# Reciprocal roots of both token tiles taken ahead of the rotations, in a two-layer hybrid decoder

## The chip, the core and the metric

The kernel runs on one core of a Trainium2 chip. The metric is the device time of one execution in microseconds (us), lower is better. PE is the matrix engine (TensorE), DVE the vector engine, ACT the scalar engine, POOL the GpSimd engine and SP the sync engine, which here only issues transfers. Each engine works through its own list of instructions in order and waits at semaphores for what the others deliver.

## What is computed

Two decoder layers over 256 tokens and 1024 channels in float32. Each layer has two attention branches (mixer A with a top-k selection of keys by a small indexer, mixer B with two softmax maps whose weighted difference is used), a gated merge, a convolutional feed-forward block and a gated embedding. Cut to what matters here:

```
qa, ka, va, qi, ki, wi, qb, kb, vb, gate_a, gate_b = split(rms_norm(h) @ w_in)
qa = rope(rms_norm(qa, g_qa));  ka = rope(rms_norm(ka, g_ka))     # heads of 64
qi = rope(qi);  ki = rope(ki);  wi = wi * H_I**-0.5 * D_I**-0.5
qb = rope(rms_norm(qb, g_qb));  kb = rope(rms_norm(kb, g_kb))
iscore = sum_h relu(qi . ki) * wi, causal;   sel = top 64 keys of each query
o_a = softmax over the selected keys (qa . ka / 8) @ va
o_b = (softmax(q1 . k1 / 8) - lam * softmax(q2 . k2 / 8)) @ vb;   o_b = rms_norm(o_b)
mix = sigmoid(gate_a) * (o_a @ w_branch_a) + sigmoid(gate_b) * (o_b @ w_branch_b)
h = h + mix @ w_out;   h = h + conv_ffn(rms_norm(h));   h = h + ple_gate * (p @ w_ple_proj)
```

The norm of a head is a sum of 64 squares and a reciprocal root. The rotation (`rope`) is linear, so the factor can be put on before or after it.

## The kernel before

**Tiles.** The 256 tokens are two tiles of 128 partitions, i = 0 and 1. All weights come in 128 chunks of 128x1024 per layer. SP issues their transfers (`raw`), ACT rounds each to a high part `wh` (line 164), DVE takes the rest `wl = raw - wh` (line 179). Every product of activations and weights is then three matmuls on PE (lines 352 to 354): `u_hi wh`, `u_hi wl`, `u_lo wh`. Here those three are called a triple. A chunk serves four triples in the projections.

**The side work.** While PE streams the projections and gates of a layer, the attention is done between its triples. Each piece is a Python generator (`index_side`, `heads_side`, `select_side`, `mixer_b`, `mixer_a`, `o_side`). A planner (`Side.tick`, called after every four triples) lets each generator go on to its next `yield`, when its own estimates of the engines' loads allow it. The three numbers of a `yield` are those estimates, for PE, DVE and ACT. They do not reach the chip. They only decide behind which triples a piece's instructions are written, and each engine then runs its list in exactly that order. Below, a visit is such a place in PE's list, named by the number of triples of the layer that stand ahead of it.

**Around the change.** A projection's result is read by ACT from PSUM to `prq` (line 477). `heads_side` works on it, for queries of mixer B, keys of mixer B (`nm == "kb"`) and queries of mixer A. For each tile `head_ss` squares on ACT (line 414) and sums on DVE (line 415, `hss`); `rpow` makes the reciprocal root on POOL (lines 261 and 262, `pw` and `rq`); `rope_rows` rotates with four DVE instructions (lines 402, 405 twice, 409). Queries take their factor later, in the exponential. Keys are multiplied by it on DVE (line 576) right behind the rotation of their tile. Then PE transposes both tiles (line 425, eight 128x128), and ACT copies them to `qT` (line 427).

**What comes behind.** `maps` multiplies queries and keys (mask at line 596, products at 628 or 633), reduces the maxima on DVE (lines 601 and 602, `mx`, `nb`), and takes exponentials on ACT (line 605, eight for a pair of maps). For mixer B, DVE then combines the two softmax maps (lines 642 to 645, writing `pe`), PE transposes `pe` (line 620), and multiplies by the values (line 656). The maps, the transposes and the products with values share four PSUM buffers named `tp`. `select_side` runs eight top-k rounds on DVE (lines 545 and 547), two for each `yield`.

Of the kernel before, what the change touches and what calls it, by code (L numbers as in the profile page):

```python
# [9 lines left out]
F32 = mybir.dt.float32  # L10
F32R = mybir.dt.float32r
BF16 = mybir.dt.bfloat16
AF = mybir.ActivationFunctionType
# [4 lines left out]
P = 128  # L18
# [7 lines left out]
EPS = 1e-6  # L26
# [83 lines left out]
def decoder_kernel(ctx: ExitStack, tc: tile.TileContext, x, pT, ws, fc, tb, gf, rope, out):  # L110
    nc = tc.nc
# [146 lines left out]
    def rpow(dst, src, mul, add):  # L258
        n = src.shape[-1]
        t = sm.tile([P, 8], F32, name="pw", bufs=4)  # L260
        nc.gpsimd.tensor_scalar(t[:, :n], src, mul, add, op0=ALU.mult, op1=ALU.add)
        nc.gpsimd.tensor_tensor(dst, t[:, :n], mhalf[:, :n], op=ALU.pow)  # L262
# [148 lines left out]
    def head_ss(src, n):  # L411
        sq = sm.tile([P, 8, 64], F32, name="sq", **T2)[:, :n, :]
        ss = sm.tile([P, 8], F32, name="hss", bufs=3)
        nc.scalar.activation(sq, src, AF.Square)
        nc.vector.reduce_sum(ss[:, :n], sq, axis=AX.X)
        return ss[:, :n]
# [25 lines left out]
    for l in range(DEPTH):  # L442
# [43 lines left out]

        def index_side(pi):
            kk, iq, wvs = [], [], []
            for i in range(2):
                v = pi[i]  # L490
                nc.scalar.activation(va[:, i, :], v[:, 64:128], AF.Copy)
                kki = sm.tile([P, 4, 64], F32, name="kk")
                rope_rows(kki[:, 0:2, :], v[:, 0:64].unsqueeze(1), 1, rt["ka"], i, dup=True)
                rope_rows(kki[:, 2:4, :], v[:, 384:448].unsqueeze(1), 1, rt["i"], i, dup=True)
                rk = sm.tile([P, 1], F32, name="rk")
                rpow(rk, head_ss(v[:, 0:64].unsqueeze(1), 1), 1.0 / 64, EPS)
                iqi = sm.tile([P, 4, 64], F32, name="iq")
                rope_rows(iqi, v[:, 128:384].rearrange("p (a b) -> p a b", b=64), 4, rt["i"], i)
                nc.scalar.activation(kki[:, 0:2, :], kki[:, 0:2, :], AF.Copy, scale=rk)
                wv = sm.tile([P, 4], F32, name="wv")  # L500
                nc.vector.tensor_scalar(wv, v[:, 448:452], 0.0625, None, op0=ALU.mult)
                kk.append(kki.rearrange("p a b -> p (a b)"))
                iq.append(iqi.rearrange("p a b -> p (a b)"))
                wvs.append(wv)
                yield 0.0, 2.8, 0.0
            pt = ps_tp.tile([P, 2, L], F32, name="tp")
            for j in range(2):
                for i in range(2):
                    nc.tensor.transpose(pt[:, j, i * P:(i + 1) * P], kk[i][:, j * P:(j + 1) * P], ident)
            nc.scalar.activation(kT, pt[:, 0, :], AF.Copy)  # L510
            nc.scalar.activation(kiT, pt[:, 1, :], AF.Copy)
            iqT = sm.tile([P, 2, L], F32, name="iqT", **T2)
            transposed(iq, 2, iqT)
            yield 0.9, 0.0, 1.2
            rels = []
            for i in range(2):
                S = P * (i + 1)
                rel = b4("rel")[:, :, :S]
                ps = [ps_tp.tile([P, 2, L], F32, name="tp") for _ in range(2)]
                for b in range(2):  # L520
                    for r in range(2):
                        nc.tensor.matmul(ps[r][:, b, :S], iqT[r * 64:(r + 1) * 64, b, i * P:(i + 1) * P],
                                         kiT[r * 64:(r + 1) * 64, :S], start=True, stop=True)
                for r in range(2):
                    nc.scalar.activation(rel[:, r:4:2, :], ps[r][:, :, :S], AF.Relu)
                rels.append(rel)
                yield 0.85 * (i + 1), 0.0, 0.9
            side.spawn(select_side(rels, wvs), P_TOPK)
# [32 lines left out]

        def heads_side(pr, nm, is_q):

            rows, rq = [], []
            for i in range(2):
                v = pr[i].rearrange("p (a b) -> p a b", b=64)
                q = sm.tile([P, 512], F32, name="qr", **T2)
                q3 = q.rearrange("p (a b) -> p a b", b=64)
                r_ = sm.tile([P, 8], F32, name="rq", bufs=6)
                if is_q:  # L570
                    rope_rows(q3, v, 8, rt[nm], i)
                    rpow(r_, head_ss(v, 8), 1.0, 64 * EPS)
                else:
                    rpow(r_, head_ss(v, 8), 1.0 / 64, EPS)
                    rope_rows(q3, v, 8, rt[nm], i)
                    nc.vector.tensor_mul(q3, q3, r_.unsqueeze(2).broadcast_to([P, 8, 64]))
                rows.append(q)
                rq.append(r_.rearrange("p (b r) -> p r b", r=2))
                yield 0.0, (2.8 if nm == "kb" else 2.2), 0.0
            rqs[nm] = rq  # L580
            qT[nm] = b4("qT")
            transposed(rows, 4, qT[nm])
            yield 0.9, 0.0, 1.0
            flags.add(nm)
# [459 lines left out]
```

## Time and profile before

| | before |
|---|---|
| median of three runs | 796.73 us (794.17 to 796.83) |
| the profiled execution | 797.8 us, of which 796.0 us are the span from the first to the last instruction |
| PE busy | 783.4 us, 98% of the span |
| DVE busy | 589.3 us, 74% |
| ACT busy | 503.5 us, 63% |
| POOL busy | 163.8 us, 21% |
| granted PE clock, mean | 0.999 |

All times below are from the one profiled execution and count from its first instruction. A busy share is an average: where engines work for one another in a chain, a wait can stand in a short stretch though the engine is far from full over the whole span.

### The profile page before, as it was taken

How to read it: one execution, taken by the hardware profiler on the slowest of the kernel's cores; microseconds unless marked ns; L12 is line 12 of the kernel's file. 1: busy time of each engine (PE TensorE's matmuls, PEld its weight loads, DVE VectorE, ACT ScalarE, POOL GpSimd, SP SyncE). 2: the span in 40 equal slices, each digit the busy share in tenths (PEclk: the TensorE clock that was granted, in tenths of full speed). 3: DMA queues.
4: the chain of work that ended last, by engine and by line, in shares of the span. 5: the costliest groups of instructions: out<-in, count | busy, mean ns of one | idle time of the engine just before them, and what ended most of it. 6: DMA issues, size and time to landing. Idle time of an engine off the chain costs nothing.

```text
span 796.0 us, 11725 instructions
## 1 busy us (share of the span) xinstructions
PE 783.4 (98%) x4049; PEld 646.7 (81%) x4049; DVE 589.3 (74%) x1130; ACT 503.5 (63%) x887; POOL 163.8 (21%) x162
## 2 busy tenths in 40 slices
PE   8999999999999999999999999999999999999997
PEld 6877876787888888888888778778878888888887
DVE  5987987677777778854686889768677777785643
ACT  6766657455877777643666486565468777774541
POOL 0240300010344442000123213000104444410000
PEclk9999999999999999999999999999999999999999
DMA  8654453474455556646365344446545555558421
GB/s 321 211 172 146 131 190 131 146 233 137 159 190 182 192 194 210 230 159 220 133 205 165 121 145 159 158 133 191 192 137 182 189 181 192 182 183 291 167 98 54
DMA packets 40332, 139.51 MB, mean 175 GB/s; under 512 B 4560, under 2 KB 5968, under 8 KB 40272
## 3 DMA queue, kind: packets, MB, share of 16 engines
q1 hardware_dynamic: 39408, 136.91, 51.4%
q10 hardware_dynamic: 864, 1.84, 0.8%
q8 instruction: 32, 0.52, 0.3%
q14 instruction: 28, 0.23, 0.1%
HBM read 137.69 MB, written 1.05 MB: 174 GB/s over the span
## 4 chain that ended last, share of the span: by engine, by line
PE 87%; DVE 5%; ACT 4%; POOL 1%; issue 1%; DMA 1%; SPq 0%; DVEq 0%; ACTq 0%; POOLq 0%
PE tp L821 21%; PE acc L352 11%; PE acc L354 11%; PE acc L353 11%; PE tp L822 10%; PE acc L905 5%; PE acc L903 5%; PE acc L904 5%; DVE wl L179 2%; ACT pe L605 2%; PE tp L315 2%; PE tp L620 1%; PE tp L699 1%; PE tp L656 1%; POOL rq L262 1%
## 5 line engine op out<-in xcount | busy, mean ns | idle before, releaser
L164 ACT ACTIVATE wh<-raw 128x1024 fp32r<-128x1024 f32 x254 | 264.7, 1058 | 37.1 <-PE acc L905 25.2
L821 PE MATMUL tp<-u,wh 128*128 128x512 f32 x704 | 249.6, 399 | 2.2 <-DVE u L787 2.2
L179 DVE TENSOR_TENSOR wl<-raw,wh 128x1024 fp32r<-128x1024 f32 x178 | 213.9, 1220 | 24.4 <-ACT wh L164 24.1
L822 PE MATMUL tp<-u,wl 128*128 128x256 f32 x704 | 197.7, 281 | 0.0
L821 PEld LDWEIGHTS tp<-u,wh 128*128 128x128 f32 x704 | 132.3, 188 | 36.1 <-DVE u L787 3.3
L352 PE MATMUL acc<-wh,u 128*128 128x512 f32 (+1 forms) x336 | 133.8, 398 | 0.0
L822 PEld LDWEIGHTS tp<-u,wl 128*128 128x128 f32 x704 | 133.0, 189 | 0.0
L354 PE MATMUL acc<-wh,u 128*128 128x512 f32 (+1 forms) x336 | 130.5, 388 | 0.0
L353 PE MATMUL acc<-wl,u 128*128 128x512 f32 (+1 forms) x336 | 130.5, 388 | 0.0
L176 POOL TENSOR_TENSOR wl<-raw,wh 128x512 fp32r<-128x512 f32 x76 | 98.5, 1296 | 149.4 <-DVE wl L175 71.5
L836 DVE SCALAR_TENSOR_TENSOR cv<-tp,fc,cv 128x255 f32<-128x255 f32 (+1 forms) x176 | 84.1, 478 | 3.1
L831 DVE TENSOR_TENSOR tp<-tp,cl 128x256 f32<-128x256 f32 x88 | 38.0, 432 | 50.9 <-ACT cl L829 50.9
L352 PEld LDWEIGHTS acc<-wh,u 128*128 128x128 f32 x336 | 63.1, 188 | 13.2 <-issue 0.7
L354 PEld LDWEIGHTS acc<-wh,u 128*128 128x128 f32 x336 | 63.1, 188 | 12.8
L353 PEld LDWEIGHTS acc<-wl,u 128*128 128x128 f32 x336 | 63.2, 188 | 11.7 <-DVE wl L179 0.2
L903 PE MATMUL acc<-wh,g 128*128 128x512 f32 x176 | 68.9, 391 | 0.0
L904 PE MATMUL acc<-wl,g 128*128 128x512 f32 x176 | 68.5, 389 | 0.0
L905 PE MATMUL acc<-wh,g 128*128 128x512 f32 x176 | 68.5, 389 | 0.0
L832 ACT ACTIVATE cv<-tp,fc 128x256 f32<-128x256 f32 x88 | 49.7, 565 | 24.5 <-DVE tp L831 24.0
L276 POOL TENSOR_SCALAR sst<-ss 128x2 f32<-128x2 f32 (+1 forms) x8 | 5.6, 699 | 259.2 <-ACT junk L268 259.1
L829 ACT ACTIVATE cl<-tp 128x256 f32<-128x256 f32 x88 | 33.8, 384 | 33.6 <-PE tp L822 33.3
L175 DVE TENSOR_TENSOR wl<-raw,wh 128x514 fp32r<-128x514 f32 x76 | 52.7, 693 | 0.0
(180 smaller groups left out, 1051.5 us busy)
## 6 DMA issues: line engine op xcount, KB each, us to landing
raw<-ws SPq DMA_DIRECT2D x254, 512.0 KB, 3.4
raw<-ws SPq DMA_DIRECT2D x4, 256.0 KB, 5.0
gb<-gf ACTq DMA_DIRECT2D x2, 512.0 KB, 4.5
h<-x SPq DMA_DIRECT2D x2, 256.0 KB, 4.3
h<-x SPq DMA_DIRECT2D x1, 512.0 KB, 6.6
px<-pT ACTq DMA_DIRECT2D x2, 256.0 KB, 2.8
out<-h SPq DMA_DIRECT2D x2, 256.0 KB, 2.8
out<-h SPq DMA_DIRECT2D x4, 128.0 KB, 1.8
```

The lines of the kernel that those rows point to most:

```text
L164: nc.scalar.activation(wh, raw, AF.Copy)
L176: nc.gpsimd.tensor_tensor(wl[:, b], raw[:, b], wh[:, b].bitcast(F32), op=ALU.subtract)
L179: nc.vector.tensor_sub(wl, raw, wh.bitcast(F32))
L352: nc.tensor.matmul(o, a, wh, start=q == 0, stop=False)
L353: nc.tensor.matmul(o, a, wl, start=False, stop=False)
L354: nc.tensor.matmul(o, b, wh, start=False, stop=q == nk - 1)
L821: nc.tensor.matmul(acc, wh[:, k, :], u.pair(k), start=k == 0, stop=False)
L822: nc.tensor.matmul(acc[:, 0, :], wl[:, k, :], u.hi(k), start=False, stop=k == KD - 1)
L836: nc.vector.scalar_tensor_tensor(c[:, sh:], pu[:, :L - sh], w[:, 2 - sh:3 - sh], c[:, sh:], op0=ALU.mult, op1=ALU.add)
L903: nc.tensor.matmul(acc[i], a, wh, start=k == 0, stop=False)
L904: nc.tensor.matmul(acc[i], a, wl, start=False, stop=False)
L905: nc.tensor.matmul(acc[i], b, wh, start=False, stop=k == NF - 1)
```

## The change

For mixer B's keys the squares, sums and reciprocal roots of both tiles are now asked for ahead of both rotations, and the multiplication by the root becomes a stage of its own, for both tiles together, behind a `yield` after the second rotation. In `index_side` the roots of both tiles' keys likewise stand ahead of the first rotation. Queries keep their order, and only their estimates in `yield` change. No arithmetic is added or dropped.

```diff
         def index_side(pi):
             kk, iq, wvs = [], [], []
+            rks = [sm.tile([P, 1], F32, name="rk") for _ in range(2)]
+            for rk, v in zip(rks, pi):
+                rpow(rk, head_ss(v[:, 0:64].unsqueeze(1), 1), 1.0 / 64, EPS)
             for i in range(2):
 ...
-                rk = sm.tile([P, 1], F32, name="rk")
-                rpow(rk, head_ss(v[:, 0:64].unsqueeze(1), 1), 1.0 / 64, EPS)
 ...
-                nc.scalar.activation(kki[:, 0:2, :], kki[:, 0:2, :], AF.Copy, scale=rk)
+                nc.scalar.activation(kki[:, 0:2, :], kki[:, 0:2, :], AF.Copy, scale=rks[i])
 ...
         def heads_side(pr, nm, is_q):
 
-            rows, rq = [], []
+            vs = [t.rearrange("p (a b) -> p a b", b=64) for t in pr]
+            rows = [sm.tile([P, 512], F32, name="qr", **T2) for _ in range(2)]
+            q3s = [q.rearrange("p (a b) -> p a b", b=64) for q in rows]
+            rs = [sm.tile([P, 8], F32, name="rq", bufs=6) for _ in range(2)]
+            rq = [r_.rearrange("p (b r) -> p r b", r=2) for r_ in rs]
+            if not is_q:
+                for r_, v in zip(rs, vs):
+                    rpow(r_, head_ss(v, 8), 1.0 / 64, EPS)
             for i in range(2):
-                v = pr[i].rearrange("p (a b) -> p a b", b=64)
-                q = sm.tile([P, 512], F32, name="qr", **T2)
-                q3 = q.rearrange("p (a b) -> p a b", b=64)
-                r_ = sm.tile([P, 8], F32, name="rq", bufs=6)
+                rope_rows(q3s[i], vs[i], 8, rt[nm], i)
                 if is_q:
-                    rope_rows(q3, v, 8, rt[nm], i)
-                    rpow(r_, head_ss(v, 8), 1.0, 64 * EPS)
+                    rpow(rs[i], head_ss(vs[i], 8), 1.0, 64 * EPS)
+                    yield 0.0, 2.7, 0.0
                 else:
-                    rpow(r_, head_ss(v, 8), 1.0 / 64, EPS)
-                    rope_rows(q3, v, 8, rt[nm], i)
+                    yield 0.0, 2.2 + 1.1 * (1 - i), 0.0
+            if not is_q:
+                for q3, r_ in zip(q3s, rs):
                     nc.vector.tensor_mul(q3, q3, r_.unsqueeze(2).broadcast_to([P, 8, 64]))
-                rows.append(q)
-                rq.append(r_.rearrange("p (b r) -> p r b", r=2))
-                yield 0.0, (2.8 if nm == "kb" else 2.2), 0.0
+                yield 0.0, 1.3, 0.0
             rqs[nm] = rq
             qT[nm] = b4("qT")
             transposed(rows, 4, qT[nm])
```

Four lines are added, so the lines behind the diff move by four: 576 becomes 582, 596 becomes 600, 605 becomes 609, 620 becomes 624, 628 becomes 632.

The planner reacts. **DVE, the keys of mixer B in the first layer**, from the sum of squares on: `m_...` are the halves of a rotation, `sc` the indexer's scores. Before:

```order
L415 TENSOR_REDUCE hss<-sq 128x8
L402 TENSOR_TENSOR m_668<-prq,rt_kb 128x512
L405 TENSOR_TENSOR m_669<-prq,rt_kb 128x8x32 x2
L409 TENSOR_TENSOR qr<-m_668,m_669 128x512
L576 TENSOR_TENSOR qr<-qr,rq 128x512
L179 TENSOR_TENSOR wl<-raw,wh 128x1024
L535 SCALAR_TENSOR_TENSOR sc<-rel,wv,cm 128x128
L538 SCALAR_TENSOR_TENSOR sc<-rel,wv,sc 128x128 x3
L179 TENSOR_TENSOR wl<-raw,wh 128x1024
```

And with the change, from the second tile's rotation on (both sums and the first rotation stand ahead of it, with the first tile's scores and two splits `wl` between):

```order
L402 TENSOR_TENSOR m_726<-prq,rt_kb 128x512
L405 TENSOR_TENSOR m_727<-prq,rt_kb 128x8x32 x2
L409 TENSOR_TENSOR qr<-m_726,m_727 128x512
L179 TENSOR_TENSOR wl<-raw,wh 128x1024
L536 SCALAR_TENSOR_TENSOR sc<-rel,wv,cm 128x256
L539 SCALAR_TENSOR_TENSOR sc<-rel,wv,sc 128x256 x3
L179 TENSOR_TENSOR wl<-raw,wh 128x1024
L582 TENSOR_TENSOR qr<-qr,rq 128x512 x2
L179 TENSOR_TENSOR wl<-raw,wh 128x1024
L546 MAX m_797<-sc 128x8
```

The multiplication no longer stands behind its own rotation. Two splits and the scores of both tiles have moved ahead of the second one, and top-k rounds, which stood behind the maps of mixer B before, follow soon after it.

**PE, the same layer, where the first transposes of `pe` stand.** Before, at the visit behind 96 triples, ten of them stood alone:

```order
L352 MATMUL acc<-wh,u 128x512
L353 MATMUL acc<-wl,u 128x512
L354 MATMUL acc<-wh,u 128x512
L620 MATMUL tp<-ident,pe 128x128 x10
L352 MATMUL acc<-wh,u 128x512
```

With the change, at the same visit:

```order
L352 MATMUL acc<-wh,u 128x512
L353 MATMUL acc<-wl,u 128x512
L354 MATMUL acc<-wh,u 128x512
L425 MATMUL tp<-ident,qr 128x128 x8
L624 MATMUL tp<-ident,pe 128x128 x4
L600 LDWEIGHTS identb
L600 MATMUL tp<-cmb,identb 128x2x128
```

The keys of mixer B are transposed behind 80 triples of the first layer instead of 72, and 76 of the second instead of 68 (counted from the first triple of the layer). The first maps still come four triples later. In the first layer the second pair of maps is now split over two later visits, the first map of it behind the four transposes of `pe`; in the second layer the second pair still stands four triples behind the first pair, and `pe` follows twelve triples later, with mixer A's query transposes ahead of it.

**ACT, the first layer, what stands around the exponentials** (`pe,sums`), with the change:

```order
L477 ACTIVATE prq<-acc,rstd 128x512 x2
L427 ACTIVATE qT<-tp 128x512 x2
L164 ACTIVATE wh<-raw 128x1024
L414 ACTIVATE sq<-prq 128x512
L609 ACTIVATE pe,sums<-tp,nb,rq 128x256 x4
L609 ACTIVATE pe,sums<-tp,nb,rq 128x128 x4
L164 ACTIVATE wh<-raw 128x1024
L414 ACTIVATE sq<-prq 128x512
L164 ACTIVATE wh<-raw 128x1024 x2
```

The squares of mixer A's second query tile stand behind eight exponentials and a split; before, the squares of its first tile stood so behind sixteen, and those of the second behind two more splits.

## Rows read from the trace of the kernel before

**Rows 1.** The page: span, and PE's busy time.

```profile
span 796.0 us, 11725 instructions
...
PE 783.4 (98%) x4049; PEld 646.7 (81%) x4049; DVE 589.3 (74%) x1130; ACT 503.5 (63%) x887; POOL 163.8 (21%) x162
```

**Rows 2.** PE's waits: line, awaited, us in total, times, longest.

```profile
PE tp L425 <- DVE qr L576: 1.3, 2, 1.0
PE tp L596 <- ACT pe L605: 0.9, 3, 0.5
```

**Rows 3.** PE's timeline, first layer: start us, us, instructions [idle before].

```profile
46.51 1.09 PE L425 MATMUL tp<-ident,qr 128*128 128x128 f32 x8
47.35 0.47 PE L352 MATMUL acc<-wh,u 128*128 128x512 f32 x1
...
61.09 0.28 PE L425 MATMUL tp<-ident,qr 128*128 128x128 f32 x1
...
62.31 0.47 PE L352 MATMUL acc<-wh,u 128*128 128x512 f32 x1
...
65.16 0.39 PE L596 MATMUL tp<-cmb,identb 128*128 128x256 bf16 x2
...
66.55 0.39 PE L596 MATMUL tp<-cmb,identb 128*128 128x256 bf16 x2
...
67.52 0.50 PE L352 MATMUL acc<-wh,u 128*128 128x512 f32 x1
...
70.41 0.59 PE L596 MATMUL tp<-cmb,identb 128*128 128x256 bf16 x2
...
73.34 0.50 PE L352 MATMUL acc<-wh,u 128*128 128x512 f32 x1
```

**Rows 4.** PE's timeline, second layer, the keys' transposes.

```profile
450.08 0.28 PE L425 MATMUL tp<-ident,qr 128*128 128x128 f32 x1
...
452.14 0.47 PE L352 MATMUL acc<-wh,u 128*128 128x512 f32 x1
```

**Rows 5.** DVE's timeline, first layer, both key tiles and behind.

```profile
50.23 0.69 DVE L415 TENSOR_REDUCE hss<-sq 128x8 f32<-128x512 f32 x1 [3.21 <-ACT sq L414]
...
53.38 0.69 DVE L576 TENSOR_TENSOR qr<-qr,rq 128x512 f32<-128x512 f32 x1 [0.46 <-POOL rq L262]
...
60.82 0.69 DVE L576 TENSOR_TENSOR qr<-qr,rq 128x512 f32<-128x512 f32 x1 [0.46 <-POOL rq L262]
...
64.52 2.35 DVE L179 TENSOR_TENSOR wl<-raw,wh 128x1024 fp32r<-128x1024 f32 x2
66.79 1.28 DVE L601 TENSOR_REDUCE mx<-tp 128x2 f32<-128x512 f32 x2
```

**Rows 6.** POOL's line 261, the first half of a root.

```profile
L261 POOL TENSOR_SCALAR pw<-hss x16: 198/830/1237, 26.3 to 480.0; 128x8 f32<-128x8 f32 x12, 128x1 f32<-128x1 f32 x4
```

**Rows 7.** DVE's timeline, first layer: two top-k rounds, and the split behind them.

```profile
91.11 0.61 DVE L545 MAX8 m<-sc 128x8 f32<-128x128 f32 x2
...
93.46 1.21 DVE L179 TENSOR_TENSOR wl<-raw,wh 128x1024 fp32r<-128x1024 f32 x1
```

**Rows 8.** ACT's timeline, first layer: first and ninth instruction behind the maxima, and a square.

```profile
68.39 0.56 ACT L605 ACTIVATE pe<-tp,nb,rq 128x256 f32<-128x256 f32 x1 [4.21 <-DVE nb L602]
...
72.31 1.08 ACT L164 ACTIVATE wh<-raw 128x1024 fp32r<-128x1024 f32 x1
...
79.25 0.70 ACT L414 ACTIVATE sq<-prq 128x512 f32<-128x512 f32 x1
```

**Rows 9.** DVE's timeline, first layer: that square's sum, and the first combined map's end.

```profile
79.99 0.69 DVE L415 TENSOR_REDUCE hss<-sq 128x8 f32<-128x512 f32 x1 [2.39 <-ACT sq L414]
...
81.85 0.17 DVE L642 RECIPROCAL rcp<-sums 128x4 f32<-128x4 f32 x1
```

**Rows 10.** DVE's timeline, second layer: the first key tile's sum.

```profile
438.93 0.69 DVE L415 TENSOR_REDUCE hss<-sq 128x8 f32<-128x512 f32 x1 [1.79 <-ACT sq L414]
```

## The prediction

> **What bounds the kernel now.** Read the page first: PE is busy in 783.4 of 796.0 us [rows 1]. Its work is the same before and after, so all that the change can give or take is PE's idle time in the attention stretches of the two layers, plus what small gaps hide inside the busy figure. The next view is the list of PE's own waits. Two lines belong to the code around the change: 1.3 us at the transposes of mixer B's keys, which wait for the multiplication by the root, and 0.9 us at the masks of the maps, which wait for exponentials to free a PSUM buffer [rows 2]. The third view, PE's timeline, gives the price more exactly from start to start. Eight transposes that wait for nothing take 47.35 - 46.51 = 0.84 us; those of the keys take 1.22 in the first layer [rows 3] and 2.06 in the second [rows 4]. So the wait at which the change aims is worth 0.38 + 1.22 = 1.6 us, 0.2% of the time. What else moves with it decides the sign.
>
> **The change part by part: the keys' wait.** In the first layer DVE starts the sum of the first key tile at 50.23 and ends the second multiplication at 60.82 + 0.69 = 61.51 [rows 5]. Twice it sits idle there for a root, 0.46 us each; a recorded end lies about 0.08 behind the next start (64.52 + 2.35 = 66.87 against 66.79 for two splits), so each idle time is 0.54 from start to start. The new order drops both: -1.08. It puts the second tile's scores and two splits ahead of the multiplications: one split with those scores takes 64.52 - 61.51 = 3.01, the other half of 66.79 - 64.52, so 1.14 [rows 5]. The keys are ready at 61.51 - 1.08 + 3.01 + 1.14 = 64.6. PE comes for them eight triples later than before. Twenty triples take 61.09 - 47.35 = 13.74 [rows 3], 0.687 each, so it comes at 61.09 + 5.50 = 66.6, and finds them with 2.0 us to spare. In the second layer the same sum starts at 438.93 [rows 10]: 453.3 against 450.08 + 5.50 = 455.6 [rows 4], 2.3 to spare. The wait goes in both layers: **-1.6 us**.
>
> **The roots.** Both now run behind the sums, one after the other. One is back 2.5 us after its sum (50.92 to 53.38 [rows 5]), two after 5.0, and DVE has some 11 us of other work ahead of the multiplications. They cost nothing under that cover; without it they would cost what they cost now. The index keys' roots are the same case in small, with no PE wait named after them [rows 2]: 0, at most the few tenths by which ACT gets on sooner.
>
> Here the trace and a rule can be weighed. POOL's first half of a root takes 0.198 to 1.237 us for operands of at most eight elements a partition [rows 6], so something holds POOL up, and DVE's sum and rotation in rows 5 show no such stretch. The Trainium skill, SBUF — State Buffer, section "SBUF: two separate sides", says that the vector engine's instructions with two SBUF inputs and GpSimd's take a shared port pair as an exclusive lock, the later one blocking. By the row alone the roots give way and cost nothing; by the rule's other direction rotations could be held up too, which is a rival below.
>
> **The maps.** Before, the second pair of maps took 73.34 - 70.41 = 2.93 against 67.52 - 65.16 = 2.36 for the first pair [rows 3]. The 0.9 us of rows 2 is 0.5 once and 0.2 twice; the two short ones are this pair in the two layers. In the new order DVE comes to the first pair's maxima without two splits in front of them, and in the first layer the second pair is taken apart and later. Gain: **-0.57 twice, -1.1**. The price of the new place in the first layer (the second map there can wait for the exponentials of the one just ahead) has no row; it lies between 0 and the 0.5 of rows 2, and I take 0.25.
>
> **What is late next.** The transposes of `pe` need DVE's combination of the maps. In DVE's list that stands behind the sum of mixer A's second query tile, which waits for ACT's square, which stands behind eight exponentials. The pattern is there already: at 79.99 DVE had idled 2.39 us for such a square [rows 9]; PE came late enough then.
>
> First layer, DVE from 64.6: three splits 3.4, two top-k rounds 93.46 - 91.11 = 2.35 [rows 7], sum and rotation of mixer A's first tile 53.38 - 50.23 - 0.54 = 2.61 [rows 5]: the maxima start at 72.9. From there to the first exponential 68.39 - 66.79 = 1.60 [rows 5, 8], eight exponentials 72.31 - 68.39 = 3.92, a split of ACT 1.0, and from a square to its sum 79.99 - 79.25 = 0.74 [rows 8, 9]: the sum starts at 80.2. With the combination it takes 81.85 - 79.99 = 1.86 [rows 9], and a split of DVE 1.14 stands between: `pe` is ready at 83.2. PE wants it at 66.6 + 0.84 (transposes) + 2.85 (four triples, 65.16 - 62.31) + 2.36 (pair) + 12 x 0.687 + 0.84 = 81.7 [rows 3]: **a wait of 1.5 us**.
>
> Second layer: here all four maps are in ACT's list ahead of that square, and the second pair's maxima stand behind mixer A's first sum, itself behind eight exponentials. PE ends the first map at 455.6 + 0.84 + 2.85 + 1.39 (66.55 - 65.16) = 460.7, with DVE free. Exponentials begin 1.60 later, end at 466.2; split and square bring mixer A's first sum to 467.9; it takes 0.61, then again 1.60 and 3.92 to 474.0, again 1.0 and 0.74 to 475.8, and 3.0 as above: 478.8. PE wants it at 459.3 + 2.36 + 2.85 + 2.36 + 8.24 + 0.84 = 475.9: **a wait of 2.9 us**. Both sums rest on lists in a fixed order; bounds are 0 (if the chain is two or three us quicker than my addition) and twice the sum.
>
> **Mixer A's maps** now have `o`'s transposes ahead of each of the first two, which use the same four buffers. No row shows that. Before, one of the three waits of rows 2, 0.5 us, is there. Between 0 and 1.0 per layer now; I take 0.5 in each: **+0.5**.
>
> **Sum:** -1.6 - 1.1 + 0.25 + 1.5 + 2.9 + 0.5 = **+2.4 us**. The profiled execution took 797.8, 1.1 over the median of 796.73. Carried to the median: 799.1. Splits for PE's stream are written up to five chunks ahead, 5 x 4 x 0.687 = 13.7 us, so DVE being some us later does not reach the triples.
>
> **The rivals.** About 0.5%, 4 us, is what a measurement of this kernel can tell from no change.
>
> *Only the gains show.* If the combination is ready when PE comes, both new waits, the 0.25 and mixer A's 0.5 a layer fall away: -1.6 - 1.1 - 0.5 = -3.2, 793.5. For it speaks that PE's list is planned, and that 1.5 us is little in a chain of 33 us. Against it: the square behind eight exponentials is not a matter of estimates. Chance 0.25, spread from there to no change.
>
> *Slower.* The wait for `pe` is longer than the sum. It decides from 4.4 us in both layers together to 6.0: beyond that the total passes +4. One more ACT split ahead of each square (2 x 1.0) and a late second half of the combination would do it: 4.4 + 2.0 + 1.0, total +5.4, 802.1. For it: in the second layer the chain goes through ACT and DVE twice. Against: PE's own delay in the first layer gives the rest of it room. Chance 0.15.
>
> *The port.* Rotations are blocked for the whole of both roots. The keys come 5.0 later, 3.0 more than there is to spare in the first layer and 2.7 in the second: +5.7 on top of +2.4, 804.8. That is the page's rule in its strict form; rows 5 have a sum and a rotation in 2.61 us beside a root of nearly that length, so it does not bear it out. Chance 0.03.
>
> *The keys' wait stays*, because a list moved for nothing: 796.7. The 2.0 us to spare speak against it. Chance 0.05.
>
> **How the numbers follow.** The forecast, +0.5 to +4, has 0.52. The time is its 799.1. The range goes down towards the gains alone and up to the slower rival, 794.5 to 802.5; the forecast's own is 797.2 to 800.7. Slower by over 0.5% is above 800.7: the slower rivals' 0.18 and a little of the forecast's edge, 0.20. Faster by over 0.5% is below 792.7, past the gains: 0.03. Within: 0.77.
>
> **What would show it.** Right: no PE wait for the multiplication (line 582); no DVE idle time for `rq` there; PE waits at line 624 for line 649 in both layers, behind DVE idle time for ACT's square; PE busy time within 1 us of before. Wrong: key transposes that still wait; no wait at line 624; or waits of PE for `wl`, which would mean that DVE's delay reaches the triples after all.

## The result, and the profile after

The changed kernel takes 800.83 us (median of six runs, 798.14 to 801.67), the kernel before 794.99 (six runs, 791.73 to 796.83). The ratio is 1.0071, with a 95% interval of 1.0044 to 1.0097: some 5.8 us slower. That is 0.7%, beyond what can be told from no change. The forecast was +2.4 us and 799.1, with 794.5 to 802.5 as its range.

The profiled execution took 801.18. Its page, to be held against [rows 1]:

```profile
span 799.4 us, 11725 instructions
...
PE 782.4 (98%) x4049; PEld 647.4 (81%) x4049; DVE 588.7 (74%) x1130; ACT 504.0 (63%) x887; POOL 163.7 (20%) x162
```

The number of instructions on each engine is the same, and PE's busy time is within 1 us of before. What is longer is the time in which PE waits. PE's waits (line, awaited, us in total, times, longest), against [rows 2]:

```profile
PE tp L624 <- DVE pe L649: 2.9, 2, 1.8
...
PE tp L600 <- ACT pe L609: 1.9, 3, 1.4
PE tp L600 <- DVE pe L693: 1.6, 2, 0.8
```

The keys' wait at line 425 is gone. In its place stand the wait for the combined maps (line 624), which the prediction named, and two at the masks of the maps (line 600), together 3.5 us where [rows 2] has 0.9; of each sum all but 0.2 (after) and 0.4 (before) falls on mixer A's maps. PE's timeline shows them from start to start, first layer, then second, against [rows 3, 4]:

```profile
67.17 1.04 PE L425 MATMUL tp<-ident,qr 128*128 128x128 f32 x8
67.96 0.48 PE L352 MATMUL acc<-wh,u 128*128 128x512 f32 x1
...
81.47 1.03 PE L425 MATMUL tp<-ident,qr 128*128 128x128 f32 x8
83.54 0.74 PE L624 MATMUL tp<-ident,pe 128*128 128x128 f32 x4 [1.03 <-DVE pe L649]
...
126.08 0.27 PE L600 MATMUL tp<-mk,identb 128*128 128x256 bf16 x1 [0.25 <-ACT pe L609]
127.17 0.27 PE L600 MATMUL tp<-mk,identb 128*128 128x256 bf16 x1 [0.82 <-DVE pe L693]
...
474.89 1.03 PE L425 MATMUL tp<-ident,qr 128*128 128x128 f32 x8
477.76 0.74 PE L624 MATMUL tp<-ident,pe 128*128 128x128 f32 x4 [1.84 <-DVE pe L649]
...
510.78 0.39 PE L600 MATMUL tp<-mk,identb 128*128 128x256 bf16 x2
...
513.23 0.27 PE L600 MATMUL tp<-mk,identb 128*128 128x256 bf16 x1 [1.41 <-ACT pe L609]
514.33 0.27 PE L600 MATMUL tp<-mk,identb 128*128 128x256 bf16 x1 [0.82 <-DVE pe L693]
...
515.34 0.79 PE L352 MATMUL acc<-wh,u 128*128 128x512 f32 x1
...
519.59 0.60 PE L624 MATMUL tp<-ident,pe 128*128 128x128 f32 x4
```

The keys' eight transposes take 67.96 - 67.17 = 0.79 and wait for nothing. The transposes of `pe` start 2.07 and 2.87 us behind the start of the eight ahead of them, which need 0.84 [rows 3]: waits of 1.2 and 2.0. In the second layer the third and fourth of mixer A's maps, from 510.78 to 515.34, take 4.56 us, and the four triples behind them 519.59 - 515.34 = 4.25. There the matmuls from 515.93 to 518.07 start 0.43 us apart instead of the 0.23 of other places. Busy time in windows (engines' busy us, then PEclk, the granted clock) shows PE's state there:

```profile
510.00:515.00 5.00, 2.77 (x25) 1.75 (x23) 4.90 (x13) 3.02 (x9) 0.00 (x0) 0.99 0.18 47
515.00:520.00 5.00, 5.00 (x22) 3.90 (x19) 4.57 (x17) 4.81 (x18) 0.00 (x0) 0.67 0.44 147
```

PE was idle for 2.23 of 5 us, and in the next window its granted clock is 0.67 on the mean: part of it is at the 1.2 GHz level and part at 2.4. So time is lost twice, in the wait and again in the triples behind it. The kernel before has at that place, in the second layer, the same two maps at their own visits, in PE's timeline:

```profile
511.14 0.39 PE L596 MATMUL tp<-mk,identb 128*128 128x256 bf16 x2
...
512.11 0.50 PE L352 MATMUL acc<-wh,u 128*128 128x512 f32 x1
...
515.00 0.43 PE L596 MATMUL tp<-mk,identb 128*128 128x256 bf16 x2
...
516.01 0.50 PE L352 MATMUL acc<-wh,u 128*128 128x512 f32 x1
```

That is 0.97 and 1.01 us for the pair, 1.98 together, and 2.89 and 2.90 us for the four triples behind each (512.11 to 515.00, and from 516.01 on). So this one place costs 4.56 - 1.98 = 2.6 us of waiting and 4.25 - 2.90 = 1.35 of half clock.

**Where it comes from.** DVE's timeline after, three places (first layer, then the second, then mixer A's maps there), against [rows 5, 9]:

```profile
63.99 1.29 DVE L582 TENSOR_TENSOR qr<-qr,rq 128x512 f32<-128x512 f32 x2
...
80.70 0.69 DVE L415 TENSOR_REDUCE hss<-sq 128x8 f32<-128x512 f32 x1 [1.68 <-ACT sq L414]
...
82.91 0.88 DVE L649 SCALAR_TENSOR_TENSOR pe<-pe,cf 128x256 f32<-128x256 f32 x2
...
474.92 0.69 DVE L415 TENSOR_REDUCE hss<-sq 128x8 f32<-128x512 f32 x1 [1.66 <-ACT sq L414]
...
509.74 0.75 DVE L319 SCALAR_TENSOR_TENSOR o<-tp,gsub,o 128x512 fp32r<-128x512 f32 x1 [3.97 <-ACT o L318]
510.41 1.28 DVE L605 TENSOR_REDUCE mx<-tp 128x2 f32<-128x512 f32 x2
```

And ACT's, for the same places, against [rows 8]:

```profile
80.01 0.65 ACT L414 ACTIVATE sq<-prq 128x512 f32<-128x512 f32 x1
...
509.00 0.71 ACT L318 ACTIVATE o<-tp,gsub 128x512 fp32r<-128x512 f32 x1
...
511.98 0.56 ACT L609 ACTIVATE pe<-tp,nb,rq 128x256 f32<-128x256 f32 x1 [2.27 <-DVE nb L606]
```

In both layers DVE stands idle for 1.7 us in front of a sum of mixer A's second query tile. ACT squares that tile only behind the eight exponentials and a split (in the first layer from 75.14 to 80.01), and the combination (line 649) that PE waits for stands behind the sum. At 509.74 it is another product that blocks the list. DVE was idle for 3.97 us for ACT's half of mixer B's output (`o`, line 318), which stands in ACT's list behind four exponentials, a split and two gate activations. The maxima of mixer A's second map stand in DVE's list behind that, though PE had ended its products at 507.93. So the exponentials of that map start at 511.98, the PSUM buffers come free late, and PE stands at the masks of the third and fourth map.

### The profile page after: what moved, and what is told of

It reads as the page before. It is cut to its first block, busy times and chain, and to the rows that moved or that the text cites. A ratio compares the mean times of both kernels' runs of the same rounds, so it can differ in the third digit from the quotient of the medians.

```text
span 799.4 us, 11725 instructions
## 1 busy us (share of the span) xinstructions
PE 782.4 (98%) x4049; PEld 647.4 (81%) x4049; DVE 588.7 (74%) x1130; ACT 504.0 (63%) x887; POOL 163.7 (20%) x162
## 3 DMA queue, kind: packets, MB, share of 16 engines
q10 hardware_dynamic: 864, 1.84, 0.8%
HBM read 137.69 MB, written 1.05 MB: 174 GB/s over the span
## 4 chain that ended last, share of the span: by engine, by line
PE 83%; DVE 8%; ACT 5%; DMA 1%; issue 1%; POOL 0%; SPq 0%; ACTq 0%; DVEq 0%; POOLq 0%
PE tp L825 20%; PE tp L826 10%; PE acc L352 10%; PE acc L354 10%; PE acc L353 10%; PE acc L909 5%; PE acc L907 5%; PE acc L908 5%; DVE wl L179 3%; ACT pe L609 2%; PE tp L315 1%; ACT wh L164 1%; DVE mx L605 1%; PE tp L624 1%; PE tp L703 1%
```

## The experiments

Four questions: is it the early roots or the new stage; is it the two waits found; are they two causes or one; and is it the planner's numbers that make them. The ratios are to runs of the kernel before on the same chip (medians 795.08 for index_only to a_after_o, 793.85 for qa_late, qa_late_o, stage_only and after_low, 795.58 for the last three). The last column leaves out the start of the program and the two feed-forward blocks, whose time varies from execution to execution (last section). It is the time from the first transposes of the indexer's queries (line 425, `iq`) to the first matmul of the feed-forward block, both layers added, in each run's one profiled execution. For the kernel before and the changed kernel these four rows of PE's timeline give it:

```profile
38.57 0.60 PE L425 MATMUL tp<-ident,iq 128*128 128x128 f32 x4
...
189.24 0.48 PE L821 MATMUL tp<-u,wh 128*128 128x512 f32 x1
...
424.84 0.60 PE L425 MATMUL tp<-ident,iq 128*128 128x128 f32 x4
...
581.45 0.48 PE L821 MATMUL tp<-u,wh 128*128 128x512 f32 x1
```

```profile
39.21 0.60 PE L425 MATMUL tp<-ident,iq 128*128 128x128 f32 x4
...
190.97 0.48 PE L825 MATMUL tp<-u,wh 128*128 128x512 f32 x1
...
424.23 0.60 PE L425 MATMUL tp<-ident,iq 128*128 128x128 f32 x4
...
584.87 0.48 PE L825 MATMUL tp<-u,wh 128*128 128x512 f32 x1
```

That is 150.7 + 156.6 = 307.3 before and 151.8 + 160.6 = 312.4 after: 5.1 us more.

| run | median us | ratio to before, 95% interval | attention stretches, us |
|---|---|---|---|
| index_only | 794.72 | 0.9996 [0.9975, 1.0018] | 306.2 |
| no_stage | 793.33 | 0.9978 [0.9960, 0.9996] | 305.2 |
| qa_ahead | 802.66 | 1.0109 [1.0069, 1.0149] | 316.7 |
| a_after_o | 797.08 | 1.0028 [1.0006, 1.0049] | 309.1 |
| stage_only | 801.70 | 1.0118 [1.0092, 1.0143] | 312.9 |
| after_low | 794.20 | 1.0019 [1.0001, 1.0036] | 306.3 |
| qa_late | 797.92 | 1.0057 [1.0037, 1.0077] | 310.0 |
| qa_late_o | 794.60 | 1.0004 [0.9980, 1.0028] | 306.6 |
| after_q22 | 802.39 | 1.0107 [1.0067, 1.0147] | 312.6 |
| b_q27 | 796.24 | 1.0013 [0.9990, 1.0036] | 306.2 |
| ns_late | 795.21 | 1.0006 [0.9987, 1.0026] | 305.0 |

**index_only: the index keys' part alone**, in the kernel before.

```diff
+            rks = [sm.tile([P, 1], F32, name="rk") for _ in range(2)]
+            for rk, v in zip(rks, pi):
+                rpow(rk, head_ss(v[:, 0:64].unsqueeze(1), 1), 1.0 / 64, EPS)
             for i in range(2):
...
-                rk = sm.tile([P, 1], F32, name="rk")
-                rpow(rk, head_ss(v[:, 0:64].unsqueeze(1), 1), 1.0 / 64, EPS)
...
-                nc.scalar.activation(kki[:, 0:2, :], kki[:, 0:2, :], AF.Copy, scale=rk)
+                nc.scalar.activation(kki[:, 0:2, :], kki[:, 0:2, :], AF.Copy, scale=rks[i])
```

> Only the index side's part of the change; the keys of mixer B as before, so PE's list is that of before. My theory (the time lies in where PE's side work is placed): no change against before, within 1.5 us, and PE's wait for the keys' multiplication stays at 1.0 to 1.5 us. Rival (roots asked for early cost time themselves, through POOL's port or ACT's order): some of the 5.8 us shows here, 1 to 3 us slower than before.

No change of the time that can be measured: that edit neither costs nor gives anything. The keys' wait, though, did not stay. It is 0.2 us in one, where 1.0 to 1.5 were expected, and the keys' part is that of the kernel before. What differs is one root, that of the second key tile in the second layer. DVE's multiplication there, in the kernel before and in this run:

```profile
450.66 0.69 DVE L576 TENSOR_TENSOR qr<-qr,rq 128x512 f32<-128x512 f32 x1 [1.53 <-POOL rq L262]
```

```profile
449.02 0.69 DVE L577 TENSOR_TENSOR qr<-qr,rq 128x512 f32<-128x512 f32 x1 [0.39 <-POOL rq L262]
```

POOL's two instructions for that root took 1.24 and 2.15 us in the profiled execution of the kernel before, and 0.57 and 1.69 in this one; in b_q27, whose keys' part is also that of the kernel before, they took 0.57 and 1.69 as well. So some 1.1 of the 1.6 us at which the prediction put the keys' wait stand in one trace of the three. How often an execution of the kernel before has them, and what makes that root long, the runs do not show.

**no_stage: the roots ahead, without the new stage.** The roots of both tiles stand ahead of the rotations as in the changed kernel. Both multiplications stand behind the second rotation without a `yield` between, and the numbers are those of the kernel before. PE's order is exactly that of the kernel before.

```diff
-                    yield 0.0, 2.7, 0.0
+                    yield 0.0, 2.2, 0.0
                 else:
-                    yield 0.0, 2.2 + 1.1 * (1 - i), 0.0
+                    if i == 0:
+                        yield 0.0, 2.8, 0.0
             if not is_q:
                 for q3, r_ in zip(q3s, rs):
                     nc.vector.tensor_mul(q3, q3, r_.unsqueeze(2).broadcast_to([P, 8, 64]))
-                yield 0.0, 1.3, 0.0
+                yield 0.0, 2.8, 0.0
```

> The change without its third stage: roots of both tiles ahead of both rotations, both multiplications right behind the second rotation, and the planner told the same numbers as before. PE's list is that of before, matmul for matmul. My theory: the keys' wait (0.4 and 1.2 us) goes, nothing takes its place, 0.5 to 2 us faster than before, so 6 to 8 us faster than the change. Rival (early roots cost time through POOL or DVE): the loss of 5.8 us or a good part of it stays, 2 us or more slower than before.

793.33: 1.75 us faster than the kernel before, and the interval just excludes no change. PE has no wait at line 425 any more, and its waits at the maps are as before, 0.9 us in three. The attention stretches are 2.1 us shorter than in the trace of the kernel before, but 1.0 shorter than in index_only and b_q27, where no root is long. So with PE's order kept the early roots gain 1 us, and 2 against an execution with a long root; the interval (0.3 to 3.2 us) can't tell these apart. By its median it is the fastest version here.

**qa_ahead: the squares and sums of mixer A's queries ahead of both rotations**, in the changed kernel.

```diff
+            if nm == "qa":
+                for r_, v in zip(rs, vs):
+                    rpow(r_, head_ss(v, 8), 1.0, 64 * EPS)
             for i in range(2):
                 rope_rows(q3s[i], vs[i], 8, rt[nm], i)
                 if is_q:
-                    rpow(rs[i], head_ss(vs[i], 8), 1.0, 64 * EPS)
+                    if nm != "qa":
+                        rpow(rs[i], head_ss(vs[i], 8), 1.0, 64 * EPS)
```

> The whole change, and the squares and sums of mixer A's two query tiles also ahead of their rotations, so that the second square no longer stands behind eight exponentials. PE's list is that of the change. My theory: PE's wait at the transposes of pe (1.8 and 1.1 us) falls to 0.5 us or less in all, 2 to 3 us faster than the change and still 2 to 4 slower than before, since mixer A's maps wait as they did. Rival (PE waits there for DVE's load, not for that square): the wait stays and the time is that of the change, within 1 us.

That missed. The profiled execution is the slowest of the four (808.39; the others 801.00 to 803.02). In it the wait for `pe` still is 2.9 us in two, 0.57 in the first layer and 2.34 in the second. There is a new wait of 0.7 at line 425 for DVE's rotation, and the mean granted clock falls to 0.991. In the second layer I had moved the sums to a place where ACT's squares are no earlier, behind the same eight exponentials: DVE stands 3.67 us for them ahead of the rotations instead, and holds these up too. An early place in one engine's list is no gain while the input stands late in another's.

**a_after_o: in the second layer mixer A's maps wait until mixer B's output stage is written**, in the changed kernel.

```diff
-            while not {"qa", "mask"} <= flags:
+            while not {"qa", "mask"} | ({"ob"} if l else set()) <= flags:
```

> The whole change, and in the second layer alone mixer A's maps wait in the plan for both of o's pieces, which puts two maps at one visit and two at the next, behind o's transposes and not among them, as in the first layer before. My theory: the waits between the third and fourth map of the second layer (1.4 and 0.8 us) fall to 0.7 or less in all, and the half-clock stretch behind them is gone: 2.5 to 4 us faster than the change. Rival (the half clock and the loss come from the whole of the stretch, not from this place): less than 1 us faster.

797.08, 3.75 us under the changed kernel's 800.83, or 3.4 by the ratios; the attention stretches are 3.3 shorter. Two waits of PE, and the window in which the maps now stand:

```profile
PE tp L600 <- ACT pe L609: 0.9, 3, 0.5
PE tp L600 <- DVE pe L693: 0.8, 1, 0.8
```

```profile
515.00:520.00 5.00, 4.52 (x32) 3.20 (x31) 4.21 (x13) 5.00 (x20) 0.00 (x0) 1.00 0.29 111
```

The waits at the masks lose 1.8 us, and the clock stays at the 2.4 GHz level. The place took 2.6 + 1.35 = 3.95 us more than before, and 3.3 to 3.75 came back. The wait for `pe` is untouched (2.8 us in two), so it is a cause of its own.

**stage_only: the new stage with each root at its old place**, in the changed kernel. PE's order is that of the changed kernel.

```diff
-            if not is_q:
-                for r_, v in zip(rs, vs):
-                    rpow(r_, head_ss(v, 8), 1.0 / 64, EPS)
             for i in range(2):
+                if not is_q:
+                    rpow(rs[i], head_ss(vs[i], 8), 1.0 / 64, EPS)
```

> The changed kernel with each root right ahead of its own tile's rotation, as in the kernel before, and the scaling still a stage of its own, with the changed kernel's numbers; the order on TensorE is that of the changed kernel. Theory (the loss comes with the added stage, which puts mixer A's work elsewhere among the others, not with the early roots): 799.5 to 802, as the changed kernel. Rival (the early roots themselves delay the rotations and cost the time): back to 795 to 797.

801.70, ratio 1.0118: no better than the changed kernel, with the waits at the masks of mixer A as they were and the one for `pe` longer, 3.5 us in two. The attention stretches are 0.5 us longer than in the changed kernel. The loss needs no early root.

**after_low: the changed kernel with lower numbers in its `yield`s.**

```diff
-                    yield 0.0, 2.7, 0.0
+                    yield 0.0, 2.2, 0.0
                 else:
-                    yield 0.0, 2.2 + 1.1 * (1 - i), 0.0
+                    yield 0.0, 2.0, 0.0
...
-                yield 0.0, 1.3, 0.0
+                yield 0.0, 1.0, 0.0
```

> The changed kernel with lower estimates handed to the planner: 2.0, 2.0 and 1.0 for the keys' three stages (5.0 in place of 6.8; 5.6 in the kernel before) and 2.2 for each query stage, as in the kernel before. No work is added, removed or moved within a stage. Theory (the estimates and the number of stages decide where mixer A's maps fall among mixer B's stages, and that is the loss): another order on TensorE and a time clearly away from 800.8, 793 to 798. Rival (the third stage costs what it costs, wherever it falls): 800 to 802.

794.20, 6.6 us under the changed kernel by the medians (by the ratios, 1.0019 against 1.0071, 4.1), and at most 0.36% above the kernel before. No instruction differs, only where they are written. The attention stretches are 6.1 shorter than in the changed kernel and as long as in index_only. The wait for `pe` is gone, the keys' wait is 0.2 us, and what is left of the maps' waits is this:

```profile
PE tp L600 <- ACT pe L609: 1.6, 4, 0.8
```

The third stage costs nothing by itself. Its place does.

**qa_late: the squares, sums and roots of mixer A's queries behind their transposes**, in the changed kernel. PE's order is that of the changed kernel.

```diff
                 if is_q:
-                    rpow(rs[i], head_ss(vs[i], 8), 1.0, 64 * EPS)
+                    if nm != "qa":
+                        rpow(rs[i], head_ss(vs[i], 8), 1.0, 64 * EPS)
...
             rqs[nm] = rq
+            if nm == "qa":
+                for r_, v in zip(rs, vs):
+                    rpow(r_, head_ss(v, 8), 1.0, 64 * EPS)
```

> The changed kernel with one edit: the squares, sums and reciprocal roots of both of mixer A's query tiles are issued behind the queries' transposes, no longer inside the two query stages. The order on TensorE stays that of the changed kernel. Theory (the vector engine waits for the scalar engine's squares, which stand behind eight exponentials, and so combines late): the wait of TensorE at mixer A's maps' first transposes for the combined tiles (excess 1.24 us in the first layer, 2.05 in the second) falls to at most 0.5 in each; the later maps of the second layer (0.98 and the half-clock stretch) may stay. Time about 3 us under the changed kernel, near 798. Rival (the combining itself, or the masks, is late whatever stands ahead of it): the wait stays at 2 to 3 us in sum and the time at 800 to 802.

The trace agrees with the theory. PE's first transposes of `pe` no longer wait:

```profile
80.52 1.03 PE L425 MATMUL tp<-ident,qr 128*128 128x128 f32 x8
81.39 0.60 PE L628 MATMUL tp<-ident,pe 128*128 128x128 f32 x4
```

No wait for line 653 is left in either layer. A new one stands at the first layer's map behind, 0.60 us of idle time and some 0.8 from start to start. So 3.3 - 0.8 = 2.5 us should come back, and the attention stretches are 2.4 shorter. The median is 2.9 lower. By the ratios alone, 1.0057 against 1.0071, the two intervals overlap, so the size rests on the trace and not on the runs' times.

**qa_late_o: that edit and the one of a_after_o together.**

```diff
-            while not {"qa", "mask"} <= flags:
+            while not {"qa", "mask"} | ({"ob"} if l else set()) <= flags:
```

> The kernel of the run before this one, and in the second layer mixer A's maps also wait until mixer B's output stage is issued. If the two causes add up (the squares, worth about 2 to 3 us, and the order of the maps against the output stage, 3.75 us when taken back alone): 794 to 795, as the kernel before or a little faster, with no stretch at a granted clock below 0.9 between 500 and 530 us. If they are two names for one delay, no better than the 797.1 that the output edit reached alone.

794.60, ratio 1.0004: the whole loss is back. In the attention stretches the two edits bring 3.3 and 2.4 us each by itself and 312.4 - 306.6 = 5.8 together. The two causes add up, and by the interval no third one of more than some 2 us is left.

**after_q22: the changed kernel with the queries' number as before.**

```diff
-                    yield 0.0, 2.7, 0.0
+                    yield 0.0, 2.2, 0.0
```

> The changed kernel with the query stages' estimate put back from 2.7 to 2.2; the keys' three stages keep theirs. In the resulting order for TensorE the output's transposes no longer stand between mixer A's maps, in either layer, but in the second layer the combined maps' transposes still follow right behind the queries' transposes. Theory (two losses, each tied to its place in the order): the maps' wait of the second layer falls below 0.7 us and no stretch below a granted clock of 0.9 is left there; the wait of 2 us for the combined maps stays in the second layer; time 796.5 to 798.5. Rival (the third stage alone costs it, whatever the queries' estimate): 800 to 802.

Half of it held. The output's transposes no longer stand between the maps, and that place has one wait of 0.48 us and full clock left. But the time is 802.39, where 796.5 to 798.5 was expected, and the attention stretches are as long as in the changed kernel. With ten transposes of `pe` in a row in the second layer, PE waits for three combinations one by one:

```profile
476.89 0.74 PE L624 MATMUL tp<-ident,pe 128*128 128x128 f32 x4 [0.68 <-DVE pe L649]
479.15 0.50 PE L624 MATMUL tp<-ident,pe 128*128 128x128 f32 x2 [1.51 <-DVE pe L649]
480.28 1.08 PE L624 MATMUL tp<-ident,pe 128*128 128x128 f32 x4 [0.63 <-DVE pe L649]
```

Behind them the matmuls are 0.43 us apart again, from 481.6 to 483.3. In the first layer the queries' transposes now wait, 1.4 us in two. The rival, that the third stage costs this much wherever it falls, gave the right number here, but after_low speaks against it. I had read two places of the new order and not the rest.

**b_q27: the kernel before with the queries' number of the changed kernel**, 2.7 in place of 2.2.

```diff
-                yield 0.0, (2.8 if nm == "kb" else 2.2), 0.0
+                yield 0.0, (2.8 if nm == "kb" else 2.7), 0.0
```

> The kernel before with one number changed: the query stages' estimate 2.7 in place of 2.2, no operation touched. In the resulting order for TensorE neither the output's transposes stand between mixer A's maps nor do the combined maps' transposes follow right behind the queries'. Theory (a time is lost where one of these two orders arises, and not with the higher estimate as such): 793.5 to 797, as the kernel before. Rival (the higher estimate alone costs most of the change's loss): 799 to 802.

796.24, no change that can be told, though PE's order differs from that of the kernel before. A higher number is no loss as such.

**ns_late: no_stage, and mixer A's squares behind the transposes.**

```diff
                 if is_q:
-                    rpow(rs[i], head_ss(vs[i], 8), 1.0, 64 * EPS)
+                    if nm != "qa":
+                        rpow(rs[i], head_ss(vs[i], 8), 1.0, 64 * EPS)
...
+            if nm == "qa":
+                for r_, v in zip(rs, vs):
+                    rpow(r_, head_ss(v, 8), 1.0, 64 * EPS)
```

> The version without a stage of its own for the scaling, which was faster than both, and in it the squares, sums and roots of mixer A's queries behind their transposes, as in the run that took them there in the changed kernel; the order on TensorE is that of the version without the stage. Theory (the squares cost only where the combined maps' transposes come early, which they do not here): the same as that version, 792.5 to 794.5. Rival (the vector engine's waits for the squares cost time in any order): 790.5 to 792.

795.21, a little above the 792.5 to 794.5 expected, and no gain over no_stage; the attention stretches are as long as there (305.0 and 305.2). Where PE comes for `pe` late, DVE's idle time for the squares costs nothing.

## Why the prediction was right, and which size was off

The direction and the steps held; one term was far too small. The median, 800.83, lies in the stated range, but just above the forecast's own 797.2 to 800.7, and a loss of over 0.5%, which came, had 0.20. That the range held is in part luck: its upper end was drawn for a rival that did not come, and some 4 us that the sum lacked were in part made up by the shorter wait for `pe`. And the forecast started from 796.73 for the kernel before, whose median came out at 794.99: the change itself, +5.8 against +2.4, is further off than the time, 800.83 against 799.1. Step by step, in us from start to start on PE, both layers together where nothing else is said:

| step | forecast | measured | from |
|---|---|---|---|
| keys' transposes | -1.6 | -1.7 | 0.79 twice, against 1.22 and 2.06 [rows 3, 4] |
| second pair of mixer B's maps | -0.85 | -0.55 | 2.52 (first layer, in two pieces) and 2.79, against 2.93 each |
| `pe`, first layer | +1.5 | +1.2 | 2.07 - 0.84 |
| `pe`, second layer | +2.9 | +2.0 | 2.87 - 0.84 |
| mixer A's maps | +0.5 | +3.2 | first layer 3.23 - 2.58, second 4.56 - 1.98 |
| triples at half clock behind them | none | +1.35 | 4.25 - 2.90 |
| sum | +2.4 | +5.6 (unrounded terms) | attention stretches: +5.1; medians: +5.8 |

**The keys.** Forecast: multiplications ended at 64.6, PE there at 66.6. They ended at 65.2 and PE came at 67.17, so 2.0 us to spare was right. no_stage shows that the gain is real. Its size in the forecast rests on one execution: 1.05 us of PE's wait in the second layer [rows 2, 4] follow the long root of that trace, and in index_only and b_q27, which keep the old order of the roots, only 0.2 of the keys' wait is left. Against those the early roots gave 1 us (no_stage), not 1.6.

**The roots and the port.** Both roots behind one another cost nothing, as forecast. DVE's two key rotations in the first layer, each with the instruction behind it, and POOL's second half of the first root:

```profile
52.07 0.68 DVE L402 TENSOR_TENSOR m<-prq,rt_kb 128x512 f32<-128x512 f32 x1
...
54.07 1.22 DVE L179 TENSOR_TENSOR wl<-raw,wh 128x1024 fp32r<-128x1024 f32 x1
...
57.76 0.69 DVE L402 TENSOR_TENSOR m<-prq,rt_kb 128x512 f32<-128x512 f32 x1
...
59.77 1.22 DVE L179 TENSOR_TENSOR wl<-raw,wh 128x1024 fp32r<-128x1024 f32 x1
```

```profile
51.93 1.64 POOL L262 TENSOR_TENSOR rq<-pw,mhalf 128x8 f32<-128x8 f32 x1
```

The first rotation lies beside POOL's instruction for most of its length and takes 54.07 - 52.07 = 2.00 us. The second, with POOL idle, takes 2.01. The Trainium skill, SBUF — State Buffer, section "SBUF: two separate sides", calls the shared port pair an exclusive lock that blocks whichever instruction comes second. For DVE's rotations beside these small roots no blocking shows in the trace, so the rival of the port falls. On POOL's side a root's second half takes from 1.64 to 2.51 us in this trace; what sets that is not shown.

**The wait for `pe`.** The chain was as written: sum behind square, square behind eight exponentials, combination behind the sum. In the first layer `pe` was ready 0.3 us later than the sum of the pieces said (83.5 against 83.2) and PE came 0.6 later (82.3 against 81.7); in the second it was ready 1.0 earlier (477.8 against 478.8). qa_late shows that it is this square and its sum: moved away, the wait is gone in both layers, with PE's order unchanged.

**Mixer A's maps: the step that was mis-sized.** The prediction saw that `o`'s transposes had come ahead of each of the first two maps, and priced that by the four shared PSUM buffers: 0 to 1.0 per layer, half taken. In the first layer it cost 0.65. In the second it cost 2.6, since what counts is not the place that the transposes take in the buffers but how late the lists of DVE and ACT free them. Moving the transposes also moves ACT's evacuation and DVE's remainder of `o` in between the maps' exponentials and maxima. I had costed a step that was moved by what it issues on PE alone. a_after_o, which undoes that order only, brings 3.3 to 3.75 us back.

**The clock.** No term stood for it. Behind the 2.2 us of standing at 511 to 514 came triples at the 1.2 GHz level, another 1.35; in a_after_o, without that standing, they ran at full clock.

**The rival that the wait for `pe` is longer** named nearly the right time (802.1) for the wrong reason. It needed 6.0 us or more there, and 1.2 + 2.0 = 3.2 were measured.

What stays open: which rule of the planner, step by step, turns the third stage and the numbers into this order. The runs show only that the same instructions in another order take 794.2 to 802.4.

## What to carry to other kernels

Where a planner writes the lists, an added stage or a changed estimate is a new order for everything behind it, and the order is the change: read the lists of all engines at every place that moved, and price a moved step by what it issues on the engines that evacuate and reduce, not by the matmuls alone. A product that two engines hand to and fro (square, sum; exponential, combination) should not stand in a list ahead of something that a third engine is about to need. If a wait is small, take it away with the rest of the order held still: here that gave 1 to 2 us, and with the order let go it cost 5.8. And a wait of which one profiled execution shows a microsecond should be looked for in a second one before it is priced.

## What was not expected of the hardware

**Two paces in the feed-forward stage.** PE, busy without a gap and at full granted clock, went through one and the same stretch of the program at one of two paces, in one execution of the changed kernel:

```profile
200.00:300.00 100.00, 100.00 (x579) 87.45 (x578) 78.86 (x162) 78.09 (x127) 45.43 (x35) 1.00 0.58 190
600.00:700.00 100.00, 100.00 (x568) 86.67 (x567) 77.39 (x158) 77.25 (x126) 45.85 (x36) 1.00 0.57 185
```

579 matmuls in 100 us in the first layer, 568 in the second. The whole block, from its first matmul to the last one of its down projection, takes 375.20 - 190.97 = 184.2 us in the first layer and 771.41 - 584.87 = 186.5 in the second. The 13 traces here have it 26 times, and each time it takes 184.2 to 184.3 or 186.5 to 186.6: the kernel before 186.6 in both layers, index_only 184.2 in both. This alone can put equal runs some 4.7 us apart. It is also why the two profiled spans differ by 3.4 only, where the medians differ by 5.8: the attention stretches are 5.1 longer after and the start 0.6 (39.21 against 38.57), but its first feed-forward block ran at the faster pace, 2.3 less. What sets the pace was not found.

**Waits in a row can cost twice.** Behind waits of 1.41 and 0.82 us in the second layer PE's granted clock fell to the 1.2 GHz level, and the matmuls stayed slow for 2.7 us. Elsewhere in the same execution it stayed at 1.00: behind the single wait of 1.84 us for `pe`, and behind those of 0.25 and 0.82 in the first layer. In a_after_o, with one wait of 0.48 us at that place, it stayed as well. Behind the three waits of after_q22 (0.68, 1.51, 0.63) it fell again.
